# Low weight halves by an accumulating DMA, and a rearranged final block, in a two-layer hybrid encoder on one core

## Chip, core and metric

The kernel runs on one core of one Trainium2 chip. The metric is the time of one execution on the device in microseconds (us), given as the median of several runs. Beside it stands one profiled execution with its trace.

## The reference, cut to what matters

```python
def reference(x, p, positions, ...):          # SEQ = D_MODEL = 1024, DEPTH = 2, all f32
    h = x
    for i in range(DEPTH):
        u = rmsnorm(h, ln_mix[i]) @ w_in[i]
        (c_q, c_kv, k_rope, gate_a, gq, gk, gv, lr_f, lr_b, gate_g) = split_cols(u, IN_SPLITS)
        y_mla = mla_branch(...) * silu(gate_a)      # 4 heads, softmax attention over latents
        y_gla = gla_branch(...) * silu(gate_g)      # 4 heads, gated linear attention both ways
        h = h + concatenate([y_mla, y_gla]) @ w_out[i]
        gate = sigmoid(rmsnorm(h, ple_norm[i]) @ w_ple_gate[i])
        h = h + gate * (p[i] @ w_ple_proj[i])
    return rmsnorm(h, final_norm)
```

## The kernel before

Activations lie transposed in SBUF: a tile has 128 features as partitions and 1024 tokens as columns. Every matmul on a weight is made of three in the reduced format `fp32r`: with w = wh + wl and x = xh + xl it adds wh·xh, wl·xh and wh·xl (`mm3`). So each block of weights, 128 x 512 as a rule, has to be split into a high half `wh` and a low half `wl`. There are 192 such blocks.

`load_split` does that. SyncE (SP) loads the raw block from HBM into `wr` (a ring of 2 buffers), ScalarE (ACT) copies it rounded into `wh` (L141), and GpSimd (POOL) writes `wl` = `wr` - `wh` (L142). `wh` and `wl` have rings of 5 buffers each, so at most five blocks stand ready, and a buffer comes free when TensorE (PE) has used the block five places earlier. One block feeds 24 matmuls of 512 columns as a rule.

The strings in `ORDER` give the program order of the steps of a layer: Q, K, G, C, D, A are input projections with what follows them, Z the decays of a gated-linear head (two scans, several exponentials), S its chain of states (L451) and scores, O its output, s, b, w attention scores, attention and output projection. A scheduler of the framework then orders the instructions on each engine; each engine runs its queue in that order. The VectorE (DVE) takes nearly all elementwise work, POOL the low halves, some products with gates (L402, L495, L789, L828) and the softmax scaling (L670).

At the end of layer 2 the tokens are cut into two blocks, `TAIL`, of 736 and 288. For each block, eight feature tiles pass through the gate: matmuls (L820), `gt` = product with 1/rms (L823, DVE), sigmoid (ACT), product with `pj` (L828; POOL, or DVE for the last two tiles of the last block), the sum into `h` (L830, DVE), square (L834, ACT) and the sum of squares `acc` (L836, DVE). When all eight are done, `rstd` sums `acc` over features by matmuls with ones (L176) and makes 1/rms on the DVE (L179 to L196); then the block's eight tiles are scaled in place, four by POOL (L843, after L838 on the DVE), four by the DVE (L845), and stored (L847). `rstd` called with a pair (`acc`, `g`) multiplies in full f32; called with one tile it first splits it into two `fp32r` parts, `sqh` (ACT) and `sql` (DVE).

Two pools of buffers matter here: `mt` (ring of 41, 128 x 1024) and `st` (ring of 3, 128 x 1024), from which `gt` comes.

Of the kernel before, what the change touches and what calls it, by code (L numbers as in the profile page):

```python
# [10 lines left out]
F32 = mybir.dt.float32  # L11
# [3 lines left out]
AF = mybir.ActivationFunctionType  # L15
ALU = mybir.AluOpType
# [3 lines left out]
P = 128  # L20
S = 1024
D = 1024
# [13 lines left out]

KEEP = (4, 5, 6, 7)

POOL_END = (0, 3, 4, 6)


V_LN, V_QN, V_KVN, V_ON, V_PN, V_BG, V_LAYER = 0, 8, 11, 13, 14, 22, 26
V_FIN = DEPTH * V_LAYER
# [8 lines left out]
ORDER = ("K0 R0 Q0 G0+ Z0 V0 K1 S0 Z1 V1 O0 S1 Q1 D0 Z2 G1 G2 P0 O1 S2 C0 Z3 D1 C1 N0 D2 O2 S3 G3 M0 A0 O3 X0 A1 E0 A2 A3+ H0 k0 T0 s0 v0 H2 k1+ s1 k2 b0 H1 k3 s2 y1 b1 H3+ s3 b2 v1 s4 y0 y3 b3 y2 s5 b4 w0 w1+ s6 w2 b5 w3+ s7 w4 b6 w5+ s8 w6 w7 b7",  # L52
         "Q0 K0 Z0 V0 S0 Z1 V1 S1 Q1 K1 Z2 G0 O0 S2 G1 Z3 G2+ C0 O1 D0 O2 S3 G3 C1 N0 D1 D2+ O3 M0 X0 A0 A1 E0 A2 k0 y2 H0 A3 T0 s0 v0 H3 k1+ s1 H1 b0 H2 s2 k2 b1 s3 y0 k3+ b2 v1 s4 y3 y1 b3 s5 b4 w0 w1+ s6 w2+ b5 w3 s7 w4 b6 w5+ s8 w6+ w7 b7")

ENG = dict(at="V", qi="V", qb="P", og="P", gate="P", sq="V", wlo="P", kT="A", put="A", o="A", ple="A", hadd="V")
TCKW = {"schedule_with_timeline_sim": True}


# [1 line left out]
def hybrid_encoder(ctx: ExitStack, tc: tile.TileContext, xT, pT, pos, vecs, w_in, wq, wk, wv,  # L60
                   wz, w_out, w_gate, w_proj, outT, dbg=None):
    nc = tc.nc
# [30 lines left out]
    vec = cp.tile([P, NV], F32, name="vec")  # L93


    def bank2(tag="mm"):
        return pp.tile([P, 2, HC], F32, tag=tag, name="ps")

    def on(site):
        return {"P": nc.gpsimd, "V": nc.vector}[ENG[site]]  # L100

    def copy(site, dst, src):
        if ENG[site] == "A":
            nc.scalar.activation(dst, src, AF.Copy)  # L104
        else:
            nc.vector.tensor_copy(dst, src)


    other = [False]

    def pick(tag):
        return {"mm": "aux", "aux": "mm"}[tag] if other[0] else tag

# [3 lines left out]
    def st(shape=(P, S), dt=F32, name="st"):  # L117
        return sp.tile(list(shape), dt, tag="st", name=name)

    def mt(dt=F32, name="mt"):  # L120
        return rp.tile([P, S], dt, tag="r", name=name)
# [5 lines left out]
    def split(hi, lo, src):  # L127
        nc.scalar.activation(hi, src, AF.Copy)  # L128
        nc.vector.tensor_tensor(lo, src, hi.bitcast(F32), op=ALU.subtract)  # L129
# [4 lines left out]

    def load_split(src, n, dst=None):

        raw = wp.tile([P, HC], F32, tag="wr", name="wr", bufs=BUFS[2])
        hi, lo = dst or (wp.tile([P, HC], F32R, tag=t, name=t, bufs=BUFS[3]) for t in ("wh", "wl"))
        with tc.high_priority():
            nc.sync.dma_start(raw[:, :n], src)  # L140
        nc.scalar.activation(hi[:, :n], raw[:, :n], AF.Copy)  # L141
        on("wlo").tensor_tensor(lo[:, :n], raw[:, :n], hi[:, :n].bitcast(F32), op=ALU.subtract)  # L142
        return hi, lo

    def load_w8(src, keep=False):
# [128 lines left out]
    sq = SquareSum()  # L274
    for k in range(8):
        raw = mt(name="xraw")
        nc.sync.dma_start(raw, xT[k])
        hi, lo = mt(F32R, "x0h"), mt(F32R, "x0l")
# [4 lines left out]
    for L in range(DEPTH):  # L283
# [336 lines left out]
        def make_k(h):  # L620
            hi, lo = load_split(wk[L, h], 2 * P)
            ps = bank2(pick("mm"))
            mm3(ps, [(hi[:, k * P:(k + 1) * P], lo[:, k * P:(k + 1) * P]) for k in range(2)], lat["C"])
            kh, kll = mt(F32R, "kh"), mt(F32R, "kll")
            split(kh, kll, flat(ps))
            return kh, kll
# [46 lines left out]
        def new_part():  # L673
            return (cp.tile([P, 4], F32, tag="top", name="top", bufs=3),
                    cp.tile([P, 4], F32, tag="sums", name="sums", bufs=4), [])
# [49 lines left out]
        hs = {}  # L725
        kk, vs, pending = {}, [], {}
        ys = [None] * 8
        for w in ORDER[L].split():
            u = int(w[1])
            other[0] = w.endswith("+")  # L730
            h, c = divmod(u, 2)
            if w[0].isupper():
                step(w[0], u)
            elif w[0] == "k":
                kk[u] = make_k(u)
            elif w[0] == "v":
                vs += make_v(u)
            elif w[0] == "s":

                part, halves = new_part(), []  # L740
                for b in range(4):
                    if u < 8:
                        score_rows(h, c, b, part)
                    if u:
                        turn(pending[u - 1][0], b, pending[u - 1][1])
                pending[u] = part, halves
            elif w[0] == "b":
                attend(h, c, *pending.pop(u), vs[h])
            elif w[0] == "y":
                raw = st(name="yraw")  # L750
                nc.sync.dma_start(raw, ygd[u])
                hi, lo = mt(F32R, "yh"), mt(F32R, "yl")
                split(hi, lo, raw)
                ys[4 + u] = (hi, lo)
            elif w[0] == "w":
                out_part(u, 1, WTAG)
# [3 lines left out]
        for j in range(4):  # L760
            hi, lo = mt(F32R, "yh"), mt(F32R, "yl")
# [3 lines left out]
        sq = SquareSum()  # L765
        for t in range(8):
# [3 lines left out]
            hi, lo = mt(F32R, "hh"), mt(F32R, "hl")  # L770
# [7 lines left out]
        if not last_layer:  # L778
            xs = []
            sq = SquareSum()  # L780
            for t in range(8):
                ps = bank2()
                mm3(ps, load_w8(w_gate[L, t]), gh)
                g = st(name="gt")
                nc.vector.tensor_tensor(g, flat(ps), r_h, op=ALU.mult)
                nc.scalar.activation(g, g, AF.Sigmoid)
                pj = st(name="pj")
                nc.sync.dma_start(pj, projd[L][t])
                on("gate").tensor_tensor(g, g, pj, op=ALU.mult)  # L789
                on("hadd").tensor_tensor(hs[t], hs[t], g, op=ALU.add)  # L790
                nc.sync.dma_start(h1d[t], hs[t])
                sq.add(hs[t])
                hi, lo = mt(F32R, "xh"), mt(F32R, "xl")
                g1 = vec[:, V_LAYER * (L + 1) + V_LN + t:V_LAYER * (L + 1) + V_LN + t + 1]
                split_gain(hi, lo, hs[t], g1)
                xs.append((hi, lo))
        else:

            kept = {}
            for w in TAIL:  # L800
                n = w.stop - w.start
                k = -(-n // HC)
                m = n // k

                def cut(t):
                    return t.rearrange("p (c m) -> p c m", m=m)

                last_block = w.stop == S
                acc = mt(name="acc")[:, :n]
                todo = [t for t in range(8) if t not in kept] + list(kept)  # L810
                for at, t in enumerate(todo):
                    ps = bank2("aux" if at % 2 else "mm")[:, :k, :m]
                    ws = kept[t] if t in kept else load_w8(w_gate[L, t], t in KEEP)
                    if t in KEEP:
                        kept[t] = ws
                    for i in range(8):
                        for j, (a, b) in enumerate(((ws[i][0], gh[i][0]), (ws[i][1], gh[i][0]),
                                                    (ws[i][0], gh[i][1]))):
                            for c in range(k):
                                nc.tensor.matmul(ps[:, c, :], lhsT=a, rhs=cut(b[:, w])[:, c, :],  # L820
                                                 start=(i == 0 and j == 0), stop=(i == 7 and j == 2))
                    g = st(name="gt")[:, :n]
                    nc.vector.tensor_tensor(cut(g), ps, cut(r_h[:, w]), op=ALU.mult)  # L823
                    nc.scalar.activation(g, g, AF.Sigmoid)
                    pj = mt(name="pj")[:, :n]
                    nc.sync.dma_start(pj, projd[L][t][:, w])
                    eng = nc.vector if last_block and at > 5 else nc.gpsimd
                    eng.tensor_tensor(g, g, pj, op=ALU.mult)  # L828
                    hw = hs[t][:, w]
                    nc.vector.tensor_tensor(hw, hw, g, op=ALU.add)  # L830
                    if at == 0:
                        nc.scalar.activation(acc, hw, AF.Square)
                    else:
                        nc.scalar.activation(g, hw, AF.Square)  # L834
                        if at < 7:
                            nc.vector.tensor_tensor(acc, acc, g, op=ALU.add)  # L836
                    if at in POOL_END:
                        nc.vector.tensor_scalar(hw, hw, vec[:, V_FIN + t:V_FIN + t + 1], None, op0=ALU.mult)  # L838
                r_f = rstd((acc, g), D, n=n)
                for at, t in enumerate(todo):  # L840
                    hw = hs[t][:, w]
                    if at in POOL_END:
                        nc.gpsimd.tensor_tensor(hw, hw, r_f[:, :n], op=ALU.mult)  # L843
                    else:
                        nc.vector.scalar_tensor_tensor(hw, hw, vec[:, V_FIN + t:V_FIN + t + 1], r_f[:, :n],  # L845
                                                       op0=ALU.mult, op1=ALU.mult)
                    nc.sync.dma_start(outT[t][:, w], hw)  # L847


# [80 lines left out]
```

## Time and profile before

| | |
|---|---|
| median of 3 runs | 1482.35 us (1480.93 to 1482.83) |
| profiled execution, its own time | 1483.45 us |
| its span, first to last instruction | 1481.7 us |
| TensorE busy | 1387.9 us, 94% of the span |
| VectorE, ScalarE, GpSimd busy | 929.8, 625.7, 573.4 us |
| mean granted TensorE clock | 0.975 |

The profiled execution's own time is 1.75 us more than its span. Busy time is the time in which an engine executes instructions; waiting is not in it. The granted clock is the share of full speed that TensorE was given.

### The profile page before, as it was taken

Reading aid. Unit: us, or ns where it says so; the run is one execution under the profiler, and the core shown is the slowest. Engines: PE = TensorE matmul, PEld = TensorE weight load, DVE = VectorE, ACT = ScalarE, POOL = GpSimd, SP = SyncE. Lnnn points to the kernel's source line nnn. Section 1 sums busy time; section 2 is a strip of 40 time slices with the busy share of each in tenths; the row PEclk is TensorE's granted clock in tenths of the full one; section 3 lists DMA queues with packets and bytes.
Section 4 is the critical chain, followed back from the end, with each engine's and each line's share of the span. In section 5 each row is a group of like instructions: output and inputs, shape, how many; then the busy total and the mean of one; then the engine's idle time right before and its main releaser. Section 6 shows DMA issues by size and latency. Waiting matters only on the chain. (4 is left out here: it accounts for less than half of the span.)

```text
span 1481.7 us, 20880 instructions
## 1 busy us (share of the span) xinstructions
PE 1387.9 (94%) x8404; PEld 1173.7 (79%) x8404; DVE 929.8 (63%) x1244; ACT 625.7 (42%) x828; POOL 573.4 (39%) x334
## 2 busy tenths in 40 slices
PE   8999899889889999999999989989989999999994
PEld 6799678678678888878889877768777888878994
DVE  2687856688655645465557878676755664447548
ACT  6454364443344534343444444623333543235331
POOL 4542332321264545223452323222334645412564
PEclk9999999999999999999999999999999999999997
DMA  8321213112501031112432121111350021211333
GB/s 293 116 74 51 62 66 144 33 51 81 157 27 57 15 100 50 64 43 86 152 134 65 37 72 51 36 54 37 121 143 29 29 71 50 71 45 55 124 103 122
DMA packets 51296, 117.51 MB, mean 79 GB/s; under 512 B 6592, under 2 KB 11584, under 8 KB 51200
## 3 DMA queue, kind: packets, MB, share of 16 engines
q1 hardware_dynamic: 51200, 116.19, 23.9%
q8 instruction: 66, 1.08, 0.3%
q14 instruction: 30, 0.25, 0.1%
HBM read 82.34 MB, written 25.43 MB: 73 GB/s over the span
## 5 line engine op out<-in xcount | busy, mean ns | idle before, releaser
L142 POOL TENSOR_TENSOR wl<-wr,wh 128x512 fp32r<-128x512 f32 (+2 forms) x184 | 270.3, 1472 | 690.0 <-ACT wh L141 615.8
L141 ACT ACTIVATE wh<-wr 128x512 fp32r<-128x512 f32 (+2 forms) x184 | 111.4, 610 | 336.9 <-PE ps L162 217.4
L670 POOL TENSOR_SCALAR sc<-sc,sums 128x1024 f32<-128x1024 f32 x64 | 181.9, 2851 | 91.4 <-DVE sums L669 76.8
L129 DVE TENSOR_TENSOR el<-ps,eh 128x1024 fp32r<-128x1024 f32 x64 | 78.0, 1221 | 47.2 <-ACT eh L128 46.4
L668 ACT ACTIVATE sc<-ps,top 128x1024 f32<-128x1024 f32 x64 | 71.4, 1116 | 82.5 <-DVE top L666 78.5
L162 PE MATMUL ps<-xh,wh 128*128 128x512 f32 x288 | 93.7, 406 | 12.2 <-DVE gate L357 5.9
L451 DVE SCALAR_TENSOR_TENSOR s<-s,last 64x128 f32<-64x128 f32 x208 | 84.6, 407 | 32.6 <-ACT s L104 25.7
L665 DVE TENSOR_REDUCE top<-ps 128x1 f32<-128x1024 f32 x64 | 78.2, 1223 | 39.8 <-PE ps L662 39.7
L162 PE MATMUL ps<-x0h,wh 128*128 128x512 f32 x288 | 93.1, 405 | 7.3 <-DVE gate L357 3.8
L162 PE MATMUL ps<-xh,wl 128*128 128x512 f32 x288 | 92.5, 400 | 0.0
L162 PE MATMUL ps<-x0h,wl 128*128 128x512 f32 x288 | 92.2, 400 | 0.0
L162 PE MATMUL ps<-xl,wh 128*128 128x512 f32 x288 | 91.7, 398 | 0.0
L162 PE MATMUL ps<-x0l,wh 128*128 128x512 f32 x288 | 91.5, 399 | 0.0
L162 PE MATMUL ps<-yh,wh 128*128 128x512 f32 x256 | 80.7, 392 | 0.9 <-DVE h L722 0.9
L162 PE MATMUL ps<-yl,wh 128*128 128x512 f32 x256 | 79.5, 390 | 0.0
L162 PE MATMUL ps<-yh,wl 128*128 128x512 f32 x256 | 79.3, 390 | 0.0
L128 ACT ACTIVATE eh<-ps 128x1024 fp32r<-128x1024 f32 x64 | 65.3, 1022 | 31.7 <-PE ps L683 30.1
L162 PEld LDWEIGHTS ps<-xh,wh 128*128 128x128 f32 x288 | 55.3, 195 | 25.3 <-DVE gate L357 6.4
L162 PEld LDWEIGHTS ps<-x0h,wh 128*128 128x128 f32 x288 | 55.2, 194 | 19.9 <-DVE gate L357 4.3
L683 PE MATMUL ps<-ident,sc 128*128 128x128 f32 x512 | 66.2, 273 | 4.6 <-DVE ql L129 3.0
L683 PEld LDWEIGHTS ps<-ident,sc 128*128 128x128 f32 x512 | 59.2, 140 | 13.0 <-DVE ql L129 3.5
L162 PEld LDWEIGHTS ps<-x0h,wl 128*128 128x128 f32 x288 | 55.8, 194 | 12.2
(251 smaller groups left out, 3499.3 us busy)
## 6 DMA issues: line engine op xcount, KB each, us to landing
wr<-in_w_in SPq DMA_DIRECT2D x88, 256.0 KB, 2.6
wr<-in_w_gate SPq DMA_DIRECT2D x40, 256.0 KB, 2.6
projd<-po SPq DMA_DIRECT2D x16, 512.0 KB, 3.7
wr<-in_w_out SPq DMA_DIRECT2D x32, 256.0 KB, 2.6
xraw<-in_xT SPq DMA_DIRECT2D x8, 512.0 KB, 4.8
gqk<-gqk SPq DMA_DIRECT2D x16, 256.0 KB, 3.0
ygd<-o SPq DMA_DIRECT2D x8, 512.0 KB, 2.6
gad<-gate SPq DMA_DIRECT2D x8, 512.0 KB, 3.0
```

The lines of the kernel that those rows point to most:

```text
L128: nc.scalar.activation(hi, src, AF.Copy)
L129: nc.vector.tensor_tensor(lo, src, hi.bitcast(F32), op=ALU.subtract)
L141: nc.scalar.activation(hi[:, :n], raw[:, :n], AF.Copy)
L142: on("wlo").tensor_tensor(lo[:, :n], raw[:, :n], hi[:, :n].bitcast(F32), op=ALU.subtract)
L162: nc.tensor.matmul(ps[:, c, :], lhsT=a, rhs=b[:, c * HC:(c + 1) * HC], start=(i == 0 and j == 0), stop=(i == n - 1 and j == 2))
L451: nc.vector.scalar_tensor_tensor(state(n)[rows], state(m)[rows], alpha[rows, m:m + 1], state(n)[rows], op0=ALU.mult, op1=ALU.add)
L665: nc.vector.tensor_reduce(m, flat(ps), axis=AX.X, op=ALU.max, negate=True)
L668: nc.scalar.activation(e, flat(ps), AF.Exp, bias=m, scale=SCALE, accum_out=sums[:, b:b + 1])
L670: nc.gpsimd.tensor_scalar(e, e, sums[:, b:b + 1], None, op0=ALU.mult)
L683: nc.tensor.transpose(out=ps[:, j, b * P:(b + 1) * P], in_=e[:, kt], identity=ident)
```

## The change

`load_split`: for all blocks from step Q0 of layer 1 on (184 of 192; the first eight are as before) ACT writes `wl` = -(`wr` rounded), and then POOL issues a DMA that reads the block a second time from HBM and adds it to `wl` in place. At the end, all products with `pj` go to the DVE; the first token block's sum of squares goes into `rstd` as one tile; its eight scalings are done by the DVE, one behind each tile of the second block, into a fresh buffer `fin` of the ring `st`, from which they are stored; the second block's eight scalings are all on the DVE, in place.

```diff
-        on("wlo").tensor_tensor(lo[:, :n], raw[:, :n], hi[:, :n].bitcast(F32), op=ALU.subtract)
+        if first[0]:
+            nc.gpsimd.tensor_tensor(lo[:, :n], raw[:, :n], hi[:, :n].bitcast(F32), op=ALU.subtract)
+        else:
+            nc.scalar.activation(lo[:, :n], raw[:, :n], AF.Copy, scale=-1.0)
+            nc.gpsimd.dma_start(lo[:, :n], src, accum_op=ALU.add)
...
+            if w == "Q0":
+                first[0] = False
...
-            kept = {}
+            kept, later = {}, []
+
+            def finish(t, w, r, o=None):
+                hw = hs[t][:, w]
+                o = hw if o is None else o[:, :w.stop - w.start]
+                nc.vector.scalar_tensor_tensor(o, hw, vec[:, V_FIN + t:V_FIN + t + 1], r, op0=ALU.mult, op1=ALU.mult)
+                nc.sync.dma_start(outT[t][:, w], o)
...
-                    eng = nc.vector if last_block and at > 5 else nc.gpsimd
-                    eng.tensor_tensor(g, g, pj, op=ALU.mult)
+                    nc.vector.tensor_tensor(g, g, pj, op=ALU.mult)
...
-                        if at < 7:
+                        if at < 7 or not last_block:
                             nc.vector.tensor_tensor(acc, acc, g, op=ALU.add)
-                    if at in POOL_END:
-                        nc.vector.tensor_scalar(hw, hw, vec[:, V_FIN + t:V_FIN + t + 1], None, op0=ALU.mult)
-                r_f = rstd((acc, g), D, n=n)
-                for at, t in enumerate(todo):
-                    hw = hs[t][:, w]
-                    if at in POOL_END:
-                        nc.gpsimd.tensor_tensor(hw, hw, r_f[:, :n], op=ALU.mult)
-                    else:
-                        nc.vector.scalar_tensor_tensor(hw, hw, vec[:, V_FIN + t:V_FIN + t + 1], r_f[:, :n],
-                                                       op0=ALU.mult, op1=ALU.mult)
-                    nc.sync.dma_start(outT[t][:, w], hw)
+
+                    if later:
+                        finish(*later.pop(0), st(name="fin"))
+                if last_block:
+                    r = rstd((acc, g), D, n=n)
+                    for t in todo:
+                        finish(t, w, r[:, :n])
+                else:
+                    r = rstd(acc, D, n=n)
+                    later = [(t, w, r[:, :n]) for t in todo]
```

What moves on ScalarE is shown on the decay of one gated-linear head in layer 1 (z, a, qi, b, ref, last and d are its tiles; `ACT_TABLE_LOAD` is a load of a function table). Before:

```order
L373 ACTIVATE z<-ps,vec 128x1024
L374 ACTIVATE a<-ps,vec 128x1024
L375 ACTIVATE a<-a 128x1024
L376 ACT_TABLE_LOAD
L376 ACTIVATE a<-a 128x1024
L141 ACTIVATE wh<-wr 128x512 x2
L395 ACT_TABLE_LOAD
L395 ACTIVATE qi<-d 128x1024
```

The same place on ScalarE now:

```order
L378 ACTIVATE z<-ps,vec 128x1024
L379 ACTIVATE a<-ps,vec 128x1024
L380 ACTIVATE a<-a 128x1024
L381 ACT_TABLE_LOAD
L381 ACTIVATE a<-a 128x1024
L146 ACTIVATE wl<-wr 128x512
L142 ACTIVATE wh<-wr 128x512
L146 ACTIVATE wl<-wr 128x512
L142 ACTIVATE wh<-wr 128x512
L400 ACT_TABLE_LOAD
L400 ACTIVATE qi<-d 128x1024
```

Ahead of `qi` two copies of 128 x 512 have become four; the rest of the queue there stands as it did.

On the VectorE the end of the program is the other place: from the end of the first block's 1/rms (the transpose into `rstd`) on. Before:

```order
L196 STREAM_TRANSPOSE rstd<-nwy 128x736
L830 TENSOR_TENSOR h<-h,gt 128x288
L845 SCALAR_TENSOR_TENSOR h<-h,vec,rstd 128x736 x4
L830 TENSOR_TENSOR h<-h,gt 128x288 x2
L836 TENSOR_TENSOR acc<-acc,gt 128x288 x2
L823 TENSOR_TENSOR gt<-ps,rstd 128x288
```

And now:

```order
L201 STREAM_TRANSPOSE rstd<-nwy 128x736
L811 SCALAR_TENSOR_TENSOR fin<-h,vec,rstd 128x736
L837 TENSOR_TENSOR gt<-ps,rstd 128x288
L811 SCALAR_TENSOR_TENSOR fin<-h,vec,rstd 128x736
L841 TENSOR_TENSOR gt<-gt,pj 128x288
L843 TENSOR_TENSOR h<-h,gt 128x288
L837 TENSOR_TENSOR gt<-ps,rstd 128x288
L849 TENSOR_TENSOR acc<-acc,gt 128x288
L811 SCALAR_TENSOR_TENSOR fin<-h,vec,rstd 128x736
```

Four scalings in a row have become eight, one at a time between the steps of the second block's tiles.

## Rows read from the trace of the kernel before

**Rows 1.** The page, busy us (share of the span) xinstructions.
```profile
PE 1387.9 (94%) x8404; PEld 1173.7 (79%) x8404; DVE 929.8 (63%) x1244; ACT 625.7 (42%) x828; POOL 573.4 (39%) x334
```

**Rows 2.** The view of waits, TensorE alone: us in total, times, longest us.
```profile
PE ps L162 <- DVE gate L357: 12.5, 4, 5.9
PE ps L176 <- ACT sqh L128: 9.6, 3, 4.8
PE ps L662 <- ACT sc L668: 8.9, 7, 2.5
PE ps L477 <- DVE s L451: 4.8, 1, 4.8
```

**Rows 3.** Stretches: from:to us, busy time (instructions) by engine, granted clock, DMA share, GB/s.
```profile
179.90:186.70 6.80, 5.48 (x44) 4.65 (x45) 4.61 (x5) 2.06 (x3) 0.00 (x0) 0.50 0.47 114
1460.50:1481.80 21.30, 2.59 (x4) 1.00 (x4) 15.11 (x39) 4.20 (x10) 5.39 (x6) 0.57 0.34 126
```

**Rows 4.** Single lines: ns min/median/max of one, first to last start in us, shapes.
```profile
L399 DVE TENSOR_TENSOR gqk<-d,ref x8: 1207/2200/2304, 107.9 to 948.1; 128x1024 f32<-128x1024 f32 x8
L451 DVE SCALAR_TENSOR_TENSOR s<-s,last x208: 342/351/2436, 121.8 to 991.1; 64x128 f32<-64x128 f32 x104
L379 DVE TENSOR_TENSOR_SCAN b<-rmask,z x8: 2282/3194/3260, 93.9 to 934.9; 64x1024 f32<-64x1024 bf16 x8
L385 DVE COPY ref<-b x16: 168/174/1231, 99.5 to 940.7; 64x16 f32<-64x16 f32 x16
L830 DVE TENSOR_TENSOR h<-h,gt x16: 444/925/2471, 1388.3 to 1468.4; 128x736 f32<-128x736 f32 x8, 128x288 f32<-128x288 f32 x8
```

**Rows 5.** Timeline, two stretches: start us, us, engine, line, tiles [idle before, releaser].
```profile
169.21 1.28 POOL L142 TENSOR_TENSOR wl<-wr,wh 128x512 fp32r<-128x512 f32 x1 [2.75 <-ACT wh L141]
169.29 1.35 DVE L451 SCALAR_TENSOR_TENSOR s<-s,last,s 64x128 f32<-64x128 f32 x1
...
280.56 4.34 POOL L142 TENSOR_TENSOR wl<-wr,wh 128x512 fp32r<-128x512 f32 x2
281.45 2.31 DVE L210 TENSOR_TENSOR acc<-acc,sq 128x1024 f32<-128x1024 f32 x1
283.68 2.30 DVE L399 TENSOR_TENSOR gqk<-d,ref 128x1024 f32<-128x1024 f32 x1
288.24 1.23 DVE L210 TENSOR_TENSOR acc<-acc,sq 128x1024 f32<-128x1024 f32 x1 [1.12 <-ACT sq L209]
```

**Rows 6.** The page's groups of instructions: busy us, mean ns, idle before.
```profile
L142 POOL TENSOR_TENSOR wl<-wr,wh 128x512 fp32r<-128x512 f32 (+2 forms) x184 | 270.3, 1472 | 690.0 <-ACT wh L141 615.8
L141 ACT ACTIVATE wh<-wr 128x512 fp32r<-128x512 f32 (+2 forms) x184 | 111.4, 610 | 336.9 <-PE ps L162 217.4
```

**Rows 7.** The chain of waits, layer 2's output projection: start us, us.
```profile
1338.51 1.30 POOL wl L142
...
1343.96 1.30 POOL wl L142
```

**Rows 8.** Timeline around the weights with least time to spare.
```profile
367.05 0.42 ACT L141 ACTIVATE wh<-wr 128x256 fp32r<-128x256 f32 x1 [6.28 <-PE ps L162]
372.52 0.62 PE L162 MATMUL ps<-ch,wl 128*128 128x512 f32 x2
```

**Rows 9.** DMA issues on the page: queue, count, KB each, us to landing.
```profile
wr<-in_w_in SPq DMA_DIRECT2D x88, 256.0 KB, 2.6
```

**Rows 10.** Timeline of the end.
```profile
1433.84 1.10 PE L176 MATMUL ps<-acc,ones_r 128*128 128x512 f32 x2 [1.30 <-DVE acc L836]
...
1450.29 9.19 POOL L843 TENSOR_TENSOR h<-h,rstd 128x736 f32<-128x736 f32 x4
1450.57 9.70 DVE L845 SCALAR_TENSOR_TENSOR h<-h,vec,rstd 128x736 f32<-128x736 f32 x4
...
1468.08 1.30 PE L176 MATMUL ps<-acc,ones_r 128*128 128x288 f32 x2 [7.61 <-DVE acc L836]
...
1474.20 4.04 DVE L845 SCALAR_TENSOR_TENSOR h<-h,vec,rstd 128x288 f32<-128x288 f32 x4
```

More of the change, by code (lines that the diff above doesn't have):

```diff
@@ L37 @@
 KEEP = (4, 5, 6, 7)
-POOL_END = (0, 3, 4, 6)
 V_LN, V_QN, V_KVN, V_ON, V_PN, V_BG, V_LAYER = 0, 8, 11, 13, 14, 22, 26
@@ L53 @@
          "Q0 K0 Z0 V0 S0 Z1 V1 S1 Q1 K1 Z2 G0 O0 S2 G1 Z3 G2+ C0 O1 D0 O2 S3 G3 C1 N0 D1 D2+ O3 M0 X0 A0 A1 E0 A2 k0 y2 H0 A3 T0 s0 v0 H3 k1+ s1 H1 b0 H2 s2 k2 b1 s3 y0 k3+ b2 v1 s4 y3 y1 b3 s5 b4 w0 w1+ s6 w2+ b5 w3 s7 w4 b6 w5+ s8 w6+ w7 b7")
-ENG = dict(at="V", qi="V", qb="P", og="P", gate="P", sq="V", wlo="P", kT="A", put="A", o="A", ple="A", hadd="V")
+ENG = dict(at="V", qi="V", qb="P", og="P", gate="P", sq="V", kT="A", put="A", o="A", ple="A", hadd="V")
 TCKW = {"schedule_with_timeline_sim": True}
@@ L109, in hybrid_encoder @@
     other = [False]
+    first = [True]
     def pick(tag):
```

## The prediction

> **What bounds the kernel.** I read the busy times first: TensorE works 1387.9 us of the span, 94%, the next engine 63% [rows 1]. So all that can be won lies in the 94 us in which TensorE stands, and in the time in which it works at half clock. The view of waits says for whom it stands: VectorE and ScalarE results of the gated-linear part (gates, states, sums of squares), none of them long, a dozen in each layer [rows 2]. A low half of weights is in that view nowhere: TensorE never waited for POOL's L142. Taking that work off POOL is therefore worth nothing directly. What counts is what POOL's subtraction does to others, and what replaces it.
>
> The stretches give the second price. At 175.64 TensorE waits 4.75 us for the states L451; in the 6.8 us behind that wait its granted clock is 0.50, the lower of its two levels (1.2 of 2.4 GHz), and it is busy 5.48 us on what takes half of that at 2.4 GHz [rows 2, 3]. The mean clock of 0.975 is about 74 us at half speed (0.025 x 1482 x 2), of which the last stretch, at 0.57, holds some 18 [rows 3]; about ten stretches of 3.4 or 6.8 us lie in the body, each behind one of the longer waits.
>
> **The subtraction and the VectorE.** The same VectorE instruction takes two very different times. L399 takes 1.21 us at best and 2.20 in the median; L451 0.35 in the median and at times seven times that; the scan L379 2.28 and 3.19; a copy of 16 columns, L385, 0.17 and up to 1.23 [rows 4]. The timeline shows why: the long ones lie beside POOL. At 169.29 an L451 takes 1.35 us, and at 281.45 and 283.68 L210 and L399 take 2.31 and 2.30 beside two L142, where L210 takes 1.23 a few us later with POOL idle [rows 5]. So a subtraction costs the VectorE instruction beside it 0.5 to 1.1 us. The change removes 184 of them, 270 us of POOL's time [rows 6].
>
> Which of that is on the path? I followed each wait of TensorE over 0.9 us in both layers back through what released it, to TensorE again, and added the prolongations beside L142, never more than the wait itself. Layer 1: 2.1 us (wait at 54), 2.1 (176), 2.45 (two at 209 to 212), 2.7 (286), 2.6 (375). Layer 2: 1.0 (816), 1.8 (873), 1.0 (922), 0.9 (950), 1.05 (987), 0.7 (1068). Together 18.4 us, some twenty prolonged instructions of the kinds above. In attention and in the output projections TensorE's waits contain none. I take 12 of the 18.4: behind a shortened chain the next one is often little shorter, and a chain that passes TensorE again gives its gain only once. Bounds: 0 and 18.4.
>
> [...]
>
> The Trainium skill, "SBUF — State Buffer", section "Who interferes with whom", says that a VectorE instruction with two SBUF inputs contends with a GpSimd instruction that reads SBUF, as the L399 rows show, but also that making a DMA's descriptors on GpSimd is shut out by VectorE instructions in a two-port mode, copies and `tensor_scalar`, and the reverse. By that rule the small copies L385 would still be held up, and the 2.45 us at 209 would shrink by some 0.9, the sum to 17.5. No run before the change has a DMA issued by POOL, so the trace cannot say.
>
> **What replaces it.** *ScalarE.* 184 copies more, 0.61 us each by L141: 112 us, to 738 of 1482 [rows 6]. The engine has room, but it is in order, and in the decay chains the copies stand between exponentials: two became four ahead of `qi`, as the order shows. Such a chain carries 1 or 2 blocks; at 0.61 us on six of the chains above that is 4 to 7 us. I take 5 against the change. Bounds: 0, if the copies fall in ScalarE's own idle time, and 20 (four per head, eight heads). ScalarE already waited for TensorE to free a `wh` buffer 217 us in all [rows 6]; the new copy waits for the `wl` buffer freed at nearly the same moment, so those stalls stay.
>
> *Latency.* The low half is now ready only after a copy, an issue on POOL and a landing. A plain load of 256 KB takes 2.6 us from issue to landing [rows 9]; twice the bytes move here (block and buffer read), so I bound it by 2.6 and 5.2 us and take 4, with the issue in it. The cover is the ring: in a steady stretch a block is made every 5.44 us (1338.51, 1343.96) and needed four blocks later, 21.8 us [rows 7]. The least cover in the body is a 128 x 256 block whose buffer came free at 367.05 and whose low half TensorE takes at 372.52, 5.5 us later [rows 8]; two copies of 0.42 and 4 us just fit. Cost 0; at 5.2 us about 1.
>
> *POOL's issue.* No row has it. SyncE's issues take 0.33 to 0.43 us; the subtraction it replaces took 1.47 in the mean. Anywhere between, POOL is less busy than before: 0. POOL becomes the bound only from about 4.3 us an issue (two blocks per feature tile of 10.9 us in layer 1's gate, beside one product of 2.3 us). I add 1 us for what the VectorE still loses to POOL.
>
> **The end.** The first block's sum of squares was multiplied in f32: 1.10 us for one pair of 512 columns, where a pair in `fp32r` takes 0.62 for two such matmuls [rows 8, 10]; over 736 columns and two parts that is some 1.8 us less of TensorE. Against it stand a new copy on ScalarE and a new subtraction on the VectorE (0.8 and 0.9 us) ahead of it, but the product is now queued later among the second block's matmuls: wait about as before (1.30).
>
> Then the VectorE: four scalings in a row beside four on POOL took 9.70 us, 2.4 each, because both read SBUF; behind them the second block's steps were late, and the last sum of squares reached TensorE 7.61 us after its last gate matmul [rows 10]. A 736-wide step takes 0.93 in the median of L830 and 2.47 at most [rows 4]. Now eight of these, 7.4 us, stand on the VectorE, and six more 288-wide products of 0.46, 2.8 us: 10.2 against 9.7, but one at a time, with 1/rms, which came at 1449.8, some 1.8 us earlier (an estimate: the last product and sum lose 2 us, three small steps beside POOL 1.6, the split into two parts adds 1.75). From about 1448 the VectorE has 7.2 + 27 x 0.38 = 17.5 us of work, so the last `h` would be at 1465.5 instead of 1468.8: 3 us. The last eight scalings take 8 x 0.37 = 3.0 instead of 4.04 us, limited by SyncE's stores; 0.5. Sum 3.5, of which the 1.8 on TensorE is a part and not added. `fin` shares a ring of three with `gt`, so `gt` two tiles on waits for a store to land, 2.6 us; at 3.2 us a tile it just fits. Bounds: 6 saved if the VectorE catches up with TensorE, 2 lost if each tile waits for its store.
>
> **Sum.** -12 - 5 - 3.5 + 5 + 1 = -14.5 us. The profiled execution took 1483.45, 1.1 over the median and 0.6 over the slowest run; I apply the difference to the median: 1482.35 - 14.5, about 1468.
>
> **Rivals.** (1) *Hidden anyway*: the VectorE is freed, but ScalarE's copies and TensorE's own round trips set the chains; only the end gains, 0 to 4 us: 1480. For it: four of the eleven waits have under 40% in prolongations, and one more, 3.85 us at 327, has none. Against it: in the chain to 286 three VectorE instructions in a row are long [rows 5]. [...] (3) *ScalarE becomes late*: a copy that waits for a `wl` buffer stands ahead of exponentials and of attention's `sc`, and each of the eight heads' chains loses 1.2 to 2.5 us more than the VectorE gives: at 20 us against 16.5 won, and half clock behind longer waits, 1488. It decides from about 2.5 us per head. (4) *POOL or the DMA is the bound*: at 6 us an issue POOL needs 14.3 us for a gate tile of 10.9, 27 us over eight tiles and as much in the projections of layer 2, 1520 and more; at a latency over 20 us every block would be late. No row speaks for either size. That the change does not do what it says I rule out: the queues show 184 issues where the subtractions stood.
>
> **Numbers.** Forecast 0.57 (its own range 1456 to 1477), hidden 0.15, more than the sum 0.10, ScalarE late 0.12, POOL or DMA 0.06. No change here means within 0.2%, 3 us, about what a measurement of this kernel can tell from no change. Faster: 0.57 + 0.10 + half of hidden, 0.75; same: 0.09, with a little of (3); slower: 0.16. The range takes in most of (2) and reaches into (3): 1446 to 1488.
>
> **What would show it.** Right: L399 near 1.21 and L379 near 2.28 in the median; ScalarE busy near 735; TensorE's waits at `gate`, `sqh` and L451 shorter and its mean clock above 0.975; low halves nowhere among its waits; L811 near 0.93, and under 5 us from the last gate matmul to L176. Wrong: TensorE waiting for the DMA's landing; the VectorE's long instructions still there beside POOL's issues; ScalarE's copies as releasers of the decay chains; TensorE's waits as long as before.

## The result, and the profile after

The changed kernel took 1463.71 us (median of 4 runs, 1461.29 to 1469.09), the kernel before beside it 1482.59 (1480.93 to 1485.2). The ratio is 0.9875, 95% interval 0.9855 to 0.9895: 18.9 us faster, where 14.5 were forecast. The profiled execution has a span of 1460.8 us.

The page's busy times of the changed kernel, and from its DMA queues packets, MB and share of time:

```profile
PE 1379.5 (94%) x8400; PEld 1168.7 (80%) x8400; DVE 863.2 (59%) x1260; ACT 720.7 (49%) x1013; POOL 427.7 (29%) x312
q1 hardware_dynamic: 51200, 116.19, 26.0%
q0 software_dynamic: 26496, 46.41, 19.1%
```

Against [rows 1] the VectorE lost 67 us of busy time and ScalarE gained 95 (112 were forecast). Lines have moved by five (L399 is now L404, L379 L384, L451 L456, L385 L390); in the tail L820 is L834. The rows that answer to [rows 4], ns min/median/max:

```profile
L404 DVE TENSOR_TENSOR gqk<-d,ref x8: 1207/1224/1227, 104.0 to 926.8; 128x1024 f32<-128x1024 f32 x8
L384 DVE TENSOR_TENSOR_SCAN b<-rmask,z x8: 2282/2283/2286, 91.8 to 914.6; 64x1024 f32<-64x1024 bf16 x8
L456 DVE SCALAR_TENSOR_TENSOR s<-s,last x208: 335/351/1549, 121.2 to 970.5; 64x128 f32<-64x128 f32 x104
L390 DVE COPY ref<-b x16: 167/174/220, 96.5 to 919.5; 64x16 f32<-64x16 f32 x16
L811 DVE SCALAR_TENSOR_TENSOR fin<-h,vec,rstd x8: 974/981/985, 1428.7 to 1446.7; 128x736 f32<-128x736 f32 x8
L811 DVE SCALAR_TENSOR_TENSOR h<-h,vec,rstd x8: 509/509/517, 1453.9 to 1456.9; 128x288 f32<-128x288 f32 x8
```

The prolonged instructions are gone: L404 and the scan stand at their best time in all eight places. TensorE's waits (us in total, times, longest), answering to [rows 2]:

```profile
PE ps L667 <- ACT sc L673: 6.8, 6, 2.5
PE ps L181 <- DVE acc L849: 6.8, 1, 6.8
PE ps L167 <- DVE gate L362: 6.8, 2, 4.6
PE ps L181 <- ACT sqh L128: 5.9, 4, 3.7
PE ps L834 <- DMA wl<-in_w_gate: 4.4, 1, 4.4
PE ps L482 <- DVE s L456: 2.4, 1, 2.4
```

The gate's waits fell from 12.5 to 6.8, those for `sqh` from 9.6 to 5.9, that for the states from 4.8 to 2.4. One is new: TensorE waits 4.4 us for a low half that the DMA has not landed. Half clock did not vanish behind the shorter waits. The stretch that answers to [rows 3], in its columns, still has the lower level, 1.2 GHz, behind the wait of 2.4 us, and so has one behind a wait of 1.97 us at 902:

```profile
177.30:184.10 6.80, 5.83 (x45) 4.90 (x46) 4.27 (x4) 2.40 (x3) 0.00 (x0) 0.50 0.60 138
...
904.40:907.80 3.40, 3.40 (x9) 2.62 (x9) 1.92 (x3) 1.42 (x2) 0.00 (x0) 0.50 0.00 0
```

POOL's new issue and the plain load of the same blocks, 2.6 us before [rows 9], from the page; then, for the line of the issue, how long its DMAs take from issue to landing:

```profile
L147 POOL DMA_DIRECT2D wl<-in_w_in x84 | 72.6, 877 | 349.1 <-ACT wl L146 311.3
...
wr<-in_w_in SPq DMA_DIRECT2D x88, 256.0 KB, 3.4
```
```profile
DMA to landing us min/median/max: 3.0/4.7/7.5
```

Where the time went is seen when each trace is cut at the same four instructions: the first matmul of the first layer's gated-linear part (L343, now L348), the first gate matmul of the tail, the VectorE's transpose that begins the first token block's 1/rms (L179, now L184), and the end. Each column is the difference of two starts, in us, for the kernels of this study:

| kernel | start-up | body | gate to 1/rms | 1/rms to end |
|---|---|---|---|---|
| before | 80.8 | 1283.9 | 77.9 | 39.1 |
| changed | 80.2 | 1261.4 | 82.0 | 37.2 |
| changed, second profile | 78.9 | 1266.5 | 84.1 | 37.3 |
| DMA alone | 78.8 | 1264.6 | 84.0 | 39.8 |
| new end alone | 79.0 | 1284.3 | 78.3 | 37.3 |
| last eight blocks by POOL | 78.4 | 1267.5 | 80.5 | 37.1 |
| other order of tiles | 77.6 | 1261.8 | 83.0 | 37.2 |
| f32 pair back | 78.3 | 1265.6 | 77.9 | 37.7 |
| f32 pair and order | 80.2 | 1263.3 | 78.6 | 37.3 |
| POOL subtracts again | 82.9 | 1316.3 | 80.6 | 37.7 |
| POOL, one input | 82.8 | 1275.6 | 80.4 | 37.0 |
| negated copy twice | 83.3 | 1271.2 | 87.5 | 37.2 |
| no DMA | 78.3 | 1259.4 | 77.7 | 37.2 |
| plain DMA, no copy | 77.2 | 1259.7 | 77.4 | 37.4 |

The two profiles of the changed kernel differ by 5 us in the body, so a body is read here to about that. The body gained 17 to 22 us, where -12 - 5 + 5 + 1, or 11 us, were forecast for it; the end, forecast to gain 3.5, lost 2.3 and 4.4: the 1/rms to the end became 1.9 shorter, but the way to it 4 to 6 longer.

### The profile page after: what moved, and what is told of

Same layout as the page of the kernel before. It is cut to its first block, busy times and chain, and to the rows that moved or that the text cites. A ratio compares the mean times of both kernels' runs of the same rounds, so it can differ in the third digit from the quotient of the medians.

```text
span 1460.8 us, 21130 instructions
## 1 busy us (share of the span) xinstructions
PE 1379.5 (94%) x8400; PEld 1168.7 (80%) x8400; DVE 863.2 (59%) x1260; ACT 720.7 (49%) x1013; POOL 427.7 (29%) x312
## 5 line engine op out<-in xcount | busy, mean ns | idle before, releaser
L146 ACT ACTIVATE wl<-wr 128x512 fp32r<-128x512 f32 (+2 forms) x176 | 107.3, 610 | 311.5 <-PE ps L167 279.3
L147 POOL DMA_DIRECT2D wl<-in_w_in x84 | 72.6, 877 | 349.1 <-ACT wl L146 311.3
L456 DVE SCALAR_TENSOR_TENSOR s<-s,last 64x128 f32<-64x128 f32 x208 | 77.0, 370 | 36.8 <-ACT s L102 29.9
L167 PE MATMUL ps<-yh,wh 128*128 128x512 f32 x256 | 80.6, 392 | 0.9 <-DVE h L727 0.9
L147 POOL DMA_DIRECT2D wl<-in_w_out x32 | 27.9, 872 | 169.5 <-ACT wl L146 168.8
```

Of the source, the lines that this page charges most:

```text
L146: nc.scalar.activation(lo[:, :n], raw[:, :n], AF.Copy, scale=-1.0)
L147: nc.gpsimd.dma_start(lo[:, :n], src, accum_op=ALU.add)
L167: nc.tensor.matmul(ps[:, c, :], lhsT=a, rhs=b[:, c * HC:(c + 1) * HC], start=(i == 0 and j == 0), stop=(i == n - 1 and j == 2))
L456: nc.vector.scalar_tensor_tensor(state(n)[rows], state(m)[rows], alpha[rows, m:m + 1], state(n)[rows], op0=ALU.mult, op1=ALU.add)
```

## The experiments

**DMA alone.** The end of the kernel before, and this in `load_split`, for the same 184 blocks as in the change:

```diff
-        on("wlo").tensor_tensor(lo[:, :n], raw[:, :n], hi[:, :n].bitcast(F32), op=ALU.subtract)
...
+            nc.scalar.activation(lo[:, :n], raw[:, :n], AF.Copy, scale=-1.0)
+            nc.gpsimd.dma_start(lo[:, :n], src, accum_op=ALU.add)
```

> Low halves by the accumulating DMA, the end of the program as before. Theory (the body gained all of it, the new end lost some): the trace of the changed kernel enters the last gate 23.2 us earlier than before and then takes 2.3 us longer, so this kernel should take about 1482.5 - 23 = 1459 to 1460 us, faster than the changed kernel by 3 to 4 us. Rival (the split of the prediction: body 11, end 3.5): about 1471, slower than the changed kernel by 7 us. TensorE should start on the first tile of 736 tokens about 23 us earlier than before by the theory, 11 by the rival.

Measured: 1467.1 us, before 1484.29 beside it; ratio 0.989 (0.9874 to 0.9907), some 16 us. TensorE comes to the last gate 21.4 us earlier than before, of which the body gave 19.3, so the theory's 23 was nearer than the rival's 11. The time lies between the two forecasts all the same, because the DMA costs the old end 6.8 us, which neither had. TensorE's two waits for a sum of squares there are 7.0 and 5.4 us, 7.6 and 1.3 before [rows 10]. The gate's products are still on POOL in this kernel. One of them, the second, began 4.9 us after its sigmoid, behind an issue that itself waited for its copy; the last five of the first token block were not held up by the DMA's issues but began within 0.4 us of ScalarE's sigmoid. TensorE's waits, and such a product:

```profile
PE ps L183 <- DVE acc L845: 12.5, 2, 7.0
```
```profile
1418.79 1.76 POOL L837 TENSOR_TENSOR gt<-gt,pj 128x736 f32<-128x736 f32 x1 [5.10 <-ACT gt L833]
```

**New end alone.** Subtraction on POOL as before, the end as in the changed kernel.

> The new end alone, low halves by POOL's subtraction as before. Theory (the end lost only because TensorE stood 4.40 us for a low half that a DMA had not landed, which held up the first block's 1/rms and with it the VectorE): no such wait here, so the end gains what the prediction forecast less a little, 1479 to 1481 us. Rival (the VectorE's new queue itself is longer, eight scalings of 0.98 us and six more products): the end loses 2.3 us here too, 1485 us.

Measured: 1481.72 us against 1484.29, ratio 0.9981 (0.9972 to 0.9989): 2.8 us gained (1.6 to 4.2), body untouched. The theory holds in the time: by itself the new end gives nearly its forecast 3.5. Its one profile places only 1.4 us of that in the end (115.6 us against 117.0); the start-up is 1.8 shorter there, which repeats no better than that. The two parts' gains, 16.3 and 2.8, add up to about what the change gave, 18.9.

**Last eight blocks by POOL, and the other order of tiles.**

```diff
-        if first[0]:
+        if first[0] or own[0]:        # own[0]: the second token block
```
```diff
-                todo = [t for t in range(8) if t not in kept] + list(kept)
+                todo = [0, 1, 4, 5, 6, 7, 2, 3] if kept else list(range(8))
```

> The changed kernel, but the eight blocks of the second token block get their low halves by POOL's subtraction. Theory (the 4.40 us wait for a landing delays everything behind it, as the VectorE is busy without a break from the first block's 1/rms to the last sum): the wait goes and the time falls by 3 to 5 us, to 1459 to 1461 us; eight subtractions beside the VectorE may take back up to 1 us. Rival (the wait is hidden by the VectorE, which is the bound at the end): no change, 1463 to 1464 us.

> The changed kernel, with the second token block's tiles in the order 0, 1, 4, 5, 6, 7, 2, 3: the four tiles whose weights are kept lie between the fifth and the sixth block of the ring, so the last three low halves have some 13 us more to land. Theory: no wait of TensorE for a landing at the end, 1458 to 1461 us; the DMAs themselves stay. Rival (the VectorE is the bound there): 1463 to 1464 us.

Measured: 1460.9 us, ratio 0.9839 (0.9826 to 0.9851), and 1459.38, ratio 0.9832 (0.9819 to 0.9845), where the changed kernel has 0.9875 and, below, 0.986. The times are as the theory said, and TensorE's wait for a landing at the end is gone in both. But the way to 1/rms is only a little shorter, 80.5 us in the first against 82 and 84 in the two profiles of the changed kernel, and 83.0 in the second, where another wait stands in its place:

```profile
PE ps L181 <- ACT sqh L128: 10.2, 5, 4.3
```

The longest of these, 4.3 us, is for `sqh` in the first block's 1/rms, and the end is no shorter than the changed kernel's. So the landing is not the only thing that is late there. Where this kernel's time comes from its one profile doesn't show.

**The f32 pair back.** One part of the change undone, alone and with the other order of tiles:

```diff
-                        if at < 7 or not last_block:
+                        if at < 7:
...
-                    r = rstd(acc, D, n=n)
+                    r = rstd((acc, g), D, n=n)
```

> The changed kernel itself, beside the others on this chip: ratio to the kernel before 0.9855 to 0.9895, as measured. In the profile its start-up (to the first gated-linear head) may differ by 2 to 3 us from run to run; the sections behind it should repeat within 1 us.

> The changed kernel with one part undone: the first token block's sum of squares goes into 1/rms as the pair (acc, last square) in f32, as before, in place of one tile split into two fp32r parts. The prediction counted the fp32r form as 1.8 us less of TensorE. Theory (TensorE is not the bound there; the chain from the last tile's square to 1/rms is, and the split adds an addition of 0.93 us, a copy of 0.80 behind a copy that waits for a load, and a subtraction of 0.93 to it): 1/rms starts 3 to 5 us earlier and the kernel gains 2 to 5 us on the changed one, ratio 0.984 to 0.986. Rival (the prediction's count): it loses about 2 us, 0.989.

> The changed kernel with the pair in f32 as in the run before it, and the second token block's tiles in the order 0, 1, 4, 5, 6, 7, 2, 3. Theory (both the late 1/rms and the low half that TensorE waits for are gone): 1/rms starts some 5 us earlier after the last matmul of the first block, ratio 0.982 to 0.984, the fastest of these. Rival (the VectorE's queue behind 1/rms, 37 us, fills up whatever is won ahead of it): as the changed kernel, 0.987 to 0.988.

Measured on one chip: changed kernel 1463.66 us, 0.986 (0.9838 to 0.9882); with the pair 1460.84, 0.9832 (0.9815 to 0.9849); pair and order 1461.32, 0.9841 (0.9824 to 0.9858). The way to 1/rms is back at 77.9 and 78.6 us. TensorE now multiplies in f32 and the kernel is not slower for it. The theory names the chain of addition, copy and subtraction that the `fp32r` form puts ahead of the product, and that chain is gone; but so is TensorE's wait for a landing, although the DMA and, in the first run, the program's order of tiles are as they were. The product stands elsewhere in TensorE's queue:

```profile
1412.38 1.10 PE L181 MATMUL ps<-acc,ones_r 128*128 128x512 f32 x2 [1.36 <-DVE acc L849]
```

So the two causes were not told apart by this pair. With the split kept and no DMA the way is 78.3 us (new end alone) and 77.7 (no DMA, below): neither costs there by itself, the two together do. The intervals overlap that of the changed kernel, so a gain of 2 to 3 us is likely, not certain; the other order adds nothing to it, against the expectation. With the two kernels before them these are the quickest here that compute the whole. The sections of the changed kernel itself were expected to repeat within 1 us; the body missed that by far, as the table shows.

**POOL works beside the VectorE again.** Behind the DMA's issue, with a scratch tile `waste` that nobody reads:

```diff
+            nc.gpsimd.tensor_tensor(waste[:, :n], raw[:, :n], hi[:, :n].bitcast(F32), op=ALU.subtract)
```

and, for the second run, an operation that reads one tile in its place:

```diff
+            nc.gpsimd.tensor_scalar(waste[:, :n], raw[:, :n], vec[:, 0:1], None, op0=ALU.mult)
```

> The changed kernel, and POOL again subtracts each block's rounded half from its raw one, behind the DMA's issue, but into a scratch buffer that nobody reads; the low halves still come by DMA. Theory (the body gained because nothing slows the VectorE beside POOL's subtraction any more): the VectorE's long instructions come back (L404 2.2 us in the median, the scan 3.2), and with them 15 to 20 us: 0.997 to 1.003 of the kernel before. Rival (the gain came from elsewhere, as from low halves that are no longer queued behind POOL's products): stays at 0.988, POOL's 1.5 us more per block being hidden.

> As the run with POOL's subtraction put back into a scratch buffer, but the scratch operation reads one SBUF tile in place of two (raw block times a column). Going by POOL's softmax scaling (2.85 us for 128x1024), it takes about 1.4 us for a block, as long as the subtraction, and it holds POOL's queue and the raw buffer as long. Theory (two SBUF inputs on POOL slow the VectorE's two-input instructions; in attention the VectorE's subtractions beside POOL's one-input scaling were never long): the VectorE's instructions stay short (L404's line 1.21, the scan 2.28 in the median) and the time stays within 5 us of the changed kernel, ratio 0.986 to 0.990. Rival (the 55 us that the subtraction cost came from POOL's queue and the raw buffers that it held): ratio above 1.01, as with the subtraction.

Measured: 1519.24 us, ratio 1.0229 (1.021 to 1.0249), and 1481.18, ratio 0.9971 (0.9959 to 0.9983). The same lines in the first run and in the second:

```profile
L406 DVE TENSOR_TENSOR gqk<-d,ref x8: 1208/2198/2779, 111.4 to 976.5; 128x1024 f32<-128x1024 f32 x8
L386 DVE TENSOR_TENSOR_SCAN b<-rmask,z x8: 2281/2732/3891, 96.7 to 962.8; 64x1024 f32<-64x1024 bf16 x8
```
```profile
L406 DVE TENSOR_TENSOR gqk<-d,ref x8: 1211/1224/1430, 107.0 to 938.3; 128x1024 f32<-128x1024 f32 x8
L386 DVE TENSOR_TENSOR_SCAN b<-rmask,z x8: 2282/2283/2658, 94.5 to 925.3; 64x1024 f32<-64x1024 bf16 x8
L149 POOL TENSOR_SCALAR waste<-wr,vec x184: 913/1567/3517, 30.5 to 1430.5; 128x512 f32<-128x512 f32 x164, 128x384 f32<-128x384 f32 x12, 128x256 f32<-128x256 f32 x8
```

The prolonged instructions come back with the subtraction: six of the eight L406 take 2.2 us or more. Beside an operation as long (1.6 us in both medians) that reads one tile they mostly keep their time, for two reasons. The price is smaller where the two meet: in two of the eight places POOL's scaling had begun 0.6 to 0.7 us ahead of L406 and ran on, and L406 took 1.43 us; the scan took 2.6 to 2.7 in such places, against 3.2 and more beside the subtraction. And they meet seldom there: the scaling needs only the raw block, so the framework lets it begin at the block's landing (137 of 184 times POOL waited for that), while the subtraction stands behind the copies and mostly behind the issue. Such a meeting in the first run, and in the second:

```profile
292.11 1.99 POOL L149 TENSOR_TENSOR waste<-wr,wh 128x512 f32<-128x512 f32 x1
292.87 2.31 DVE L406 TENSOR_TENSOR gqk<-d,ref 128x1024 f32<-128x1024 f32 x1
...
151.97 1.87 POOL L149 TENSOR_SCALAR waste<-wr,vec 128x512 f32<-128x512 f32 x1
152.61 1.43 DVE L406 TENSOR_TENSOR gqk<-d,ref 128x1024 f32<-128x1024 f32 x1
```

Over the whole program the VectorE is busy 939.4 us with the subtraction, 891.6 with the scaling and 863.2 in the changed kernel, so the scaling prolongs it too, by 28 us where the subtraction does by 76. The 38 us between the two kernels are the price of the second input and of that other place in the queue together. Both expectations missed in size. The subtraction cost 55.6 us over the changed kernel, not 15 to 20, so this price, on top of ScalarE's second copy, is not the price in the kernel before. And the one-input form cost 17.5, not under 5: POOL's queue, the raw buffer held longer and what contention is left were not told apart. A part of the change's own gain may then have come through POOL's queue, and not through the VectorE; no run here separates it.

With the subtraction TensorE's waits for the gate and the states are long again, and half clock grew: 88.7 us of such stretches in the body, against 30.7 in the changed kernel and 51.2 before (sums over the trace's clock records).

```profile
PE ps L169 <- DVE gate L364: 15.6, 4, 6.9
PE ps L484 <- DVE s L458: 6.1, 1, 6.1
```

**ScalarE's copies, and the DMA, priced.** The negated copy written twice; the DMA left out; and a plain DMA in place of copy and accumulation:

```diff
+            nc.scalar.activation(lo[:, :n], raw[:, :n], AF.Copy, scale=-1.0)
```
```diff
-            nc.gpsimd.dma_start(lo[:, :n], src, accum_op=ALU.add)
```
```diff
-            nc.scalar.activation(lo[:, :n], raw[:, :n], AF.Copy, scale=-1.0)
-            nc.gpsimd.dma_start(lo[:, :n], src, accum_op=ALU.add)
+            nc.gpsimd.dma_start(lo[:, :n], src)
```

> The changed kernel with the negated copy on ScalarE written twice: 112 us more on ScalarE, as much as the change added, to some 832 us busy. By the prediction's term (the first 112 us cost 5): 4 to 7 us more than the changed kernel, ratio 0.989 to 0.992. Rival (the copies fall in ScalarE's idle time): within 2 us of it, 0.986 to 0.9875. A second rival (chains already at their limit, each further copy counts): 15 us and more, above 0.996.

> The changed kernel without the accumulating DMA: the low half is then the negated rounded block, which leaves the correction by the low half out of the product. Prices the DMA's issue and landing, with ScalarE's copies kept. The prediction put latency, issue and traffic at 0 to 1 us. Theory now: two waits of TensorE, 4.1 us at 367 and 4.4 at the second token block, come with the DMA, each with half clock behind it; without it 4 to 10 us less, ratio 0.980 to 0.984. Rival (hidden, as predicted): 0.986 to 0.987.

> The changed kernel with the low half loaded by a plain DMA from POOL's queue and no negated copy on ScalarE: the low half is then the raw block itself, so the subtraction of the high half is left out. POOL's issues, the second read of every block and its landing stay; ScalarE's 112 us and the DMA's wait for the copy go. Against the changed kernel: ScalarE's 4 to 5 us by the prediction's term, and a few more if the landing is on the path: ratio 0.981 to 0.984. Rival (the copies cost nothing): 0.986.

The last two kernels leave a part of the product out and serve only to price what is gone from them. Measured, before at 1485.31: copies twice 1480.23 us, ratio 0.9969 (0.9959 to 0.998); no DMA 1453.91, 0.9791 (0.9776 to 0.9805); plain DMA 1451.01, 0.9772 (0.9755 to 0.979). Against the changed kernel's 1463.66: +16.6 (the second rival's size, not the 4 to 7 of the prediction's term), -9.8 (at the edge of the 4 to 10 expected) and -12.7 (more than expected).

The DMA is not hidden. Without it the way to 1/rms is 77.7 us, as before the change, and the body 2 to 7 us shorter. I had expected its wait at 367 us to go too, but that one is a VectorE chain and stays. A plain DMA with no copy ahead of it leaves TensorE no wait for a landing either, and it lands in 3.1 us in the median instead of 4.7:

```profile
DMA to landing us min/median/max: 2.3/3.1/7.1
```

So the price seems to lie in the accumulating DMA behind a copy, more than in the traffic. If that plain DMA costs nothing, ScalarE's first 112 us cost the difference of the last two kernels, about 3 us (their intervals overlap); no kernel leaves out both, so this is an estimate and at the low end. The next 112 cost 16.6, with the accumulating DMA waiting behind them. A part of that is the DMA's, since the low half at the end is later still (4.4 us in the changed kernel):

```profile
PE ps L835 <- DMA wl<-in_w_gate: 7.1, 1, 7.1
```

## Why the prediction was right, and where it was not

**Mechanism: right in the main.** The VectorE was slowed by POOL's subtraction, and taking that away is the gain: L404 and L384 came out as forecast, the waits at `gate`, `sqh` and the states fell, and putting the subtraction back brought the long instructions and the long waits back, with more time than the change had won. In the trace before, the chains behind nine of the prediction's eleven waits hold VectorE and ScalarE instructions alone, as far as the releasers tell; POOL is in those at 54 and 1068. That the VectorE is the whole of it is not shown, as the scaling's 17.5 us say.

**The sum: near by luck.** The body gained 19.5 us (the mean of the seven kernels and profiles with the change's DMA and nothing put in, 1264.4, against 1283.9) where 11 were forecast, and the end lost 2.3 and 4.4 where it was to gain 3.5. The two misses have opposite signs, and so the total came near.

**The VectorE's chains (-12) and half clock (-5): too small.** With the copies gone and the DMA free to start early (the plain DMA), the body is 24.2 us shorter than before, in one profile each. Half clock stood in the body for 51.2 us before, and for 34.1 in that kernel, which is worth at most half of the difference, 8.6; some 16 are then left for the chains, between the 12 taken and the 18.4 counted. As a body repeats to about 5 us, the discount, "behind a shortened chain the next one is often little shorter", is too large by this reading but not shown to be. At one place it was right: the wait at 375 fell from 3.4 to 1.5 us, and the one behind it, at 386 before and 367 now, grew from 1.2 to 4.1.

In the changed kernel half clock stood in the body for 30.7 us (34.1 in the second profile), worth at most 10.2 us against before. No run shows what the 5 of the forecast stands on. The half clock is gone behind the waits at 54, 375 and 873, but a new stretch follows the wait at 367, and the length of a wait alone does not tell: before the change one of 1.90 us was followed by the lower level and one of 2.61 was not,

```profile
404.49 0.50 PE L662 MATMUL ps<-kh,qh 128*128 128x512 f32 x1 [1.90 <-ACT sc L668]
...
952.34 0.50 PE L176 MATMUL ps<-sqh,ones_r 128*128 128x512 f32 x1 [2.61 <-ACT sqh L128]
```
```profile
405.20:408.60 3.40, 3.40 (x10) 2.62 (x9) 0.16 (x1) 0.79 (x2) 3.40 (x2) 0.50 0.80 296
952.00:985.00 33.00, 32.66 (x341) 26.98 (x342) 24.25 (x48) 12.53 (x21) 12.97 (x9) 1.00 0.20 69
```

and in the changed kernel one of 1.56 us at 1092 and one of 1.97 at 902 were, while another of 1.97 at 487 was not. So it was also not only "the longer waits" behind which half clock stood before.

**ScalarE (+5): inside its bounds, the size open**, some 3 us by the estimate above; rival 3, ScalarE late, stood near, since the same again costs 16.6. Rival 1 (hidden anyway) fell with the body, although the count for it is wrong: by the prediction's own list three of the waits have under 40% in prolongations (922, 950, 987), not four. Rival 4 fell with the issue of 0.86 us.

**Latency (0) and issue (+1): the step that failed.** Together they cost 9.8 us, by the kernel without the DMA. The issue was in its bounds (0.86 us, between 0.33 and 1.47). The landing takes 4.7 us in the median, 7.5 at most, against 4 taken and 5.2 as the bound. Worse was the cover. That a block is made every 5.44 us and "needed four blocks later" holds where a block feeds 24 matmuls of 512 columns. In the second token block it feeds 12 of 288, one every 0.13 us, 1.6 us in all, so a ring of five covers 8 us. On top of that the scheduler put the third of these tiles ahead of the second, so the sixth block was wanted behind 36 such matmuls instead of 60. The changed kernel's timeline there:

```profile
1410.15 0.82 ACT L838 ACTIVATE gt<-gt 128x736 f32<-128x736 f32 x1 [1.89 <-DVE gt L837]
1410.87 0.61 ACT L146 ACTIVATE wl<-wr 128x512 fp32r<-128x512 f32 x1
...
1411.78 0.87 POOL L147 DMA_DIRECT2D wl<-in_w_gate  x1 [11.29 <-ACT wl L146]
...
1416.95 0.61 PE L834 MATMUL ps<-hh,wl 128*128 128x288 f32 x1 [4.40 <-DMA wl<-in_w_gate]
```

The first of the ring's buffers came free at about 1408.9 (12 matmuls behind 1407.3), but the copy stood behind a sigmoid that waited for the VectorE until 1410.15; the copy and 5.1 us from issue to landing did the rest. In the body some 5 us of the DMA's price remain, the mean of seven bodies (1264.4) over those without it; which waits hold them stays open.

**The end (-3.5): about right, but the DMA's price lies on top of it.** The new end gave 2.8 us by itself, and beside the DMA it is 2.4 to 4.5 shorter than the old one (119.3 and 121.4 us against 123.8). The DMA costs the end more than that: without it, the new end takes 115.0. In the changed kernel the first block's 1/rms begins 4.1 us later after the tail's first matmul than before, and behind it the VectorE has no time to make that up:

```profile
1423.59 0.95 DVE L184 STREAM_TRANSPOSE rstd<-ps 128x736 f32<-128x736 f32 x1 [5.49 <-PE ps L181]
...
1448.04 0.46 DVE L843 TENSOR_TENSOR h<-h,gt 128x288 f32<-128x288 f32 x1
```

Between these two rows it waits 1.0 us in 24. Two forecasts of this part were wrong: the last sum still reached TensorE 6.8 us after its last gate matmul, not under 5 (7.6 before, [rows 10]), and so it did with the new end alone, without any DMA; and the last scalings take 0.51 us each, in a row some 0.43 apart, where 0.37 was taken. The "1.8 us less of TensorE" came (the product's matmuls take 1.35 us in all, 3.20 with the f32 pair) but was no gain: beside the DMA the pair in f32 does no worse and perhaps better.

**The rule weighed in the prediction.** The small copies were not held up by POOL's issues: L390 took 0.22 us at most, the two that lay beside an issue 0.22 against 0.17. The Trainium skill, "SBUF — State Buffer", section "Who interferes with whom", would have descriptor making and such copies shut each other out; no row here shows that. Its other half, two SBUF inputs on the VectorE against a GpSimd that reads SBUF, agrees with the rows L406 of 2.2 us, and, at a smaller price, with the 1.43 us of the same line beside a one-input read that had begun first.

## What to carry to other kernels

Price an operation that stands on no critical path by what it does to its neighbours: here the body was some 20 us longer with a POOL subtraction that TensorE never waited for, in the main through the VectorE as far as the traces tell. Before a producer gets slower, compute its cover at the place where a buffer lives shortest, not in the steady stretch, and look at what the scheduler has put next there. Don't take an engine at half load for a reserve: ScalarE's first 112 us of copies cost some 3 us by estimate, the next, with a DMA waiting behind them, 16.6. And look at what else a rebuilt program moves: two kernels that differ in one line had POOL's work at different places.

## What was not expected of the hardware

- Who pays when VectorE and POOL meet depends here on who had begun. Where POOL's operation had begun 0.6 to 0.8 us ahead, the VectorE's L406 took 2.2 to 2.3 us beside a subtraction and 1.43 beside a scaling, instead of 1.21. Where the VectorE's scan had begun 0.4 to 0.9 us ahead, it kept its 2.28 us, and POOL's instruction grew instead, the subtraction from 1.6 to 2.9 us and the scaling as much. At starts within 0.15 us of each other it went either way.
- An accumulating DMA from POOL's queue lands in 4.7 us in the median, mostly 256 KB at a time, a plain one from the same queue in 3.1, and POOL's issue takes 0.86 and 0.53 us; plain loads on SyncE's queue went from 2.6 us to 3.4 beside the accumulating one and 3.2 beside the plain one.
- Two executions of the changed kernel, with the same program, differ by 5 us in the body; its timed runs spread over 8.9 us (1459.66 to 1468.53), those of the kernel before beside it over 5.3.
